# Prompt attention: score products and the steps of the sums over v traced one by one in turn

## The chip, the cores and the metric

The kernel runs on one core of a Trainium2 chip. The metric is the device time of one execution in microseconds (us). The core has five engines with a queue of instructions each: TensorE (PE, matrix products; its weight loads are listed as PEld), VectorE (DVE), ScalarE (ACT), GpSimd (POOL) and SyncE (SP, which issues most DMA transfers).

## What is computed

One inference step of a decoder with two layers, for a prompt of 2048 tokens and for 8 samples of 4 new tokens. Layer 0 joins a gated linear attention and a "forgetting" softmax attention of 4 heads of 128 channels, layer 1 is a gated linear attention. The change touches the softmax attention of the prompt alone, in the reference:

```python
def fox_prompt(q, k, v, log_f):                       # (1, 2048, 4, 128)
    c = jnp.cumsum(log_f, axis=1).swapaxes(1, 2)
    def block(args):                                  # 128 queries at a time
        qi, ci, s0 = args
        logits = einsum('bthd,bshd->bhts', qi, k) * scale + ci[..., None] - c[:, :, None, :]
        logits = where(t[:, None] >= key_pos[None, :], logits, -inf)
        p = softmax(logits, axis=-1)
        return einsum('bhts,bshd->bthd', p, v)
```

Beside it the kernel computes `fox_sample`, the same attention of the 32 sample tokens over a paged cache of 2048 past tokens for each sample.

## The kernel before

**The phase.** The program has three phases, one after the other: the input projections and linear attention of layer 0 (`phase_even`), the softmax attention (`phase_fox`, 877 to 1319 us of the profiled execution), and the output projection of layer 0 with all of layer 1 (`phase_odd`).

**Groups and blocks.** The prompt's attention goes through 16 groups (h, G): head h = 0 to 3, and in it G = 0 to 3, the 512 queries from 512 G on. A group has four blocks b = 0 to 3 of 128 queries. `scores(h, G, b)` makes G + 1 products of the block's queries with 512 keys each (the last with 128 (b + 1) keys). A number in float32 is carried as the sum of two in float16, so each product is three matmuls (`mm3`, L467 to L469). The result lies in a PSUM tile `s`, of which there are two; VectorE adds the bias, keeps the running maximum and writes the tile `L` (L1200). When the block's last product is out, the softmax follows: the negative maximum (L1206), one exponential for each `L` on ScalarE (L1208), the reciprocal of the sum on VectorE (L1211, L1212), and the normalisation of each `L` on GpSimd (L1216). `L` tiles lie in 17 buffers ("P").

**The sums over v.** `values(h, G, rows, po, b1, b2)` is a generator of steps. A full step (all four blocks, 128 keys) transposes up to four 128 x 128 pieces of `L` on TensorE into one PSUM tile `pt` (L1236), ScalarE rounds it to float16 (`th`, L1243), VectorE writes the rest (`tl`, L1244), and one `mm3` adds the product with v into the PSUM tile `po` (named fo), of which there is one. The transposes run two steps ahead of the matmuls. After the last step VectorE multiplies by the gate (`fy`, L1259) and GpSimd issues the store (L1261). A group has 4 (G + 1) such steps. The last group, (3, 3), is done in two halves, blocks 0 and 1 and then blocks 2 and 3, in 7 and 8 steps of two blocks and 256 keys each; a flag `alone`, read when a generator of sums starts, lets its transposes use two more PSUM tiles ("kt") when the sample attention is already traced.

**The order of tracing.** In a group's loop the sums of the group before (`pv`, `ns` = their number of steps) are dealt out over the blocks: for each block first `scores`, all its products and its softmax, then ns // 4 steps of `pv` (L1280 to L1283). So a block of G = 3 is traced as four products, softmax, three steps; of G = 2 as three products, softmax, two steps; of G = 1 as two, softmax, one; of G = 0 as one, softmax, and four steps of the last group of the head before. After the last block of (3, 3) come its two halves of sums, one after the other (L1288 to L1290).

**What merges with it.** Each `yield` gives a cost. `until` (L92) traces the prompt's generator and that of the sample attention so that their costs run as 270000 to 411000, until the sample's is done; the rest of the prompt is merged by `mux` (L75) with `prepare` (L1834) as 18000 to 12200. `prepare` splits the first unit of the output projection's weights into float16 (L345 to L350) and loads and splits the first two pieces, 256 tokens each, of that projection's input (L1592 to L1597).

**The engines' queues.** The order of tracing is not yet that of an engine. A planner goes through the program with costs of its own: of the instructions of an engine whose inputs and buffers it takes to be ready, it puts the one that was traced first into the queue. The chip then takes each queue in that fixed order.

Of the kernel before, what the change touches and what calls it, by code (L numbers as in the profile page):

```python
# [8 lines left out]
F32 = mybir.dt.float32  # L9
# [10 lines left out]
P = 128  # L20
# [101 lines left out]
class Kern:  # L122
# [1027 lines left out]
    def fox_prompt(self, fx, pps, caus):  # L1150
# [13 lines left out]
        def loads(h, G):  # L1164
            gs = slice(G * 512, (G + 1) * 512)
            raw["q"] = self.load(fx, self.qTd[h][:, gs], f"q{h}{G}")
            raw["k"] = self.load(fx, self.kTd[h][:, gs], f"k{h}{G}")
            bias(h, G)
            raw["v"] = self.load(fx, self.vd[gs, h * P : (h + 1) * P].rearrange("(c s) d -> s c d", s=P), f"v{h}{G}")
            SG[h, G] = fx.tile([P, 512], F32, tag="sg", name=f"fsg{h}{G}")  # L1170
            nc.sync.dma_start(SG[h, G], self.sgd[h][:, gs])

        def split(which, h, G):

            with ExitStack() as st:
                for x in (self.last_exp, self.last_kt):
                    if x is not None:
                        st.enter_context(self.tc.issue_after(x.ins))
                r = self.split(fx, raw[which], f"{which}{h}{G}", self.fsc["v", h // 2][0] if which == "v" else None)
                {"q": Q, "k": K, "v": V}[which][h, G] = r  # L1180

        def scores(h, G, b):
            tb = 4 * G + b
            cb = cbs[h]
            cm = fx.tile([P, P], F32, tag="cm", name=f"cm{h}{tb}")
            self.last_cm = nc.gpsimd.tensor_tensor(cm, cb[:, tb * P : (tb + 1) * P], caus, ALU.add)
            mx = fx.tile([P, 8], F32, tag="st1", name=f"mx{h}{tb}")
            L, na = [], 0
            q = [x[:, b * P : (b + 1) * P] for x in Q[h, G]]
            for j in range(G + 1):  # L1190
                w = 512 if j < G else (b + 1) * P
                ps = pps.tile([P, 512], F32, tag="s", name=f"s{h}{tb}{j}")
                self.last_pe = self.mm3(ps[:, :w], q, [x[:, :w] for x in K[h, j]], True, True)
                lt = fx.tile([P, 512], F32, tag="P", name=f"L{h}{tb}{j}")
                L.append((lt, w))
                parts = [(0, 512, cb[:, j * 512 : j * 512 + 512])] if j < G else \
                    ([(0, b * P, cb[:, j * 512 : j * 512 + b * P])] if b else []) + [(b * P, (b + 1) * P, cm)]
                for a, e, bs in parts:
                    init = -3e38 if na == 0 else mx[:, na - 1 : na]
                    self.last_l = nc.vector.tensor_tensor_reduce(lt[:, a:e], ps[:, a:e], bs, 1.0, init, ALU.add,  # L1200
                                                                 ALU.max, mx[:, na : na + 1])
                    na += 1
                yield 3 * w / 2.4
            nm = fx.tile([P, 8], F32, tag="st1", name=f"nm{h}{tb}")
            ib = self.logit[h // 2][0]
            nc.vector.tensor_scalar(nm[:, 0:1], mx[:, na - 1 : na], ib, -1.0, ALU.mult, ALU.mult)  # L1206
            for j, (lt, w) in enumerate(L):
                self.last_exp = nc.scalar.activation(lt[:, :w], lt[:, :w], AF.Exp, bias=nm[:, 0:1], scale=ib,  # L1208
                                                     accum_out=nm[:, 2 + j : 3 + j])
            if G:  # L1210
                nc.vector.reduce_sum(nm[:, 1:2], nm[:, 2 : 3 + G], axis=mybir.AxisListType.X)  # L1211
                nc.vector.reciprocal(nm[:, 1:2], nm[:, 1:2])  # L1212
            else:
                nc.vector.reciprocal(nm[:, 1:2], nm[:, 2:3])
            for lt, w in L:
                nc.gpsimd.tensor_scalar(lt[:, :w], lt[:, :w], nm[:, 1:2], 2.0**14, ALU.mult, ALU.mult)  # L1216
            return L

        def values(h, G, rows, po, b1, b2):

            ns, per = 4 * G + b2, 4 // (b2 - b1)
            c1, c2 = b1 * P, b2 * P
            alone = self.sample_done

            def turn(j):


                tag = "kt" if alone and j % 2 else "t"
                pt = pps.tile([P, 512], F32, tag=tag, name=f"pt{h}{G}{b1}{j}")
                w, parts = 0, []  # L1230
                for s in range(j * per, min(j * per + per, ns)):
                    b0 = max(b1, s - 4 * G)
                    w = max(w, b0 * P if per == 1 else 0)
                    parts.append((s, w, b0 * P))
                    for b in range(b0, b2):
                        nc.tensor.transpose(pt[:, w : w + P], rows[b][s // 4][0][:, (s % 4) * P : (s % 4 + 1) * P],  # L1236
                                            self.ident)
                        w += P
                th = fx.tile([P, 512], F16, tag="th", name=f"th{h}{G}{b1}{j}")
                tl = fx.tile([P, 512], F16, tag="tl", name=f"tl{h}{G}{b1}{j}")  # L1240
                a = parts[0][1]
                self.turns.append((
                    nc.scalar.activation(th[:, a:w], pt[:, a:w], AF.Copy),  # L1243
                    nc.vector.tensor_tensor(tl[:, a:w], pt[:, a:w], th[:, a:w], ALU.subtract)))  # L1244
                return th, tl, parts

            nj = -(-ns // per)
            ahead = [turn(j) for j in range(min(2, nj))]
            for j in range(nj):
                if j + len(ahead) < nj:  # L1250
                    ahead.append(turn(j + len(ahead)))
                th, tl, parts = ahead.pop(0)
                for s, a, c0 in parts:
                    vv = [x[:, (s % 4) * P : (s % 4 + 1) * P] for x in V[h, s // 4]]
                    self.last_pe = self.mm3(po[:, c0:c2], vv, [x[:, a : a + c2 - c0] for x in (th, tl)], s == 0,
                                            s == ns - 1)
                yield sum(c2 - c0 for _, _, c0 in parts) * 2.1
            y = fx.tile([P, 512], F32, tag="y", name=f"fy{h}{G}{b1}")
            nc.vector.scalar_tensor_tensor(y[:, c1:c2], po[:, c1:c2], self.v_undo[h // 2], SG[h, G][:, c1:c2], ALU.mult,  # L1259
                                           ALU.mult)  # L1260
            nc.gpsimd.dma_start(self.yT[0][NH + h][:, G * 512 + c1 : G * 512 + c2], y[:, c1:c2])  # L1261

        groups = [(h, G) for h in range(NH) for G in range(4)]
        loads(0, 0)
        for x in "qkv":
            split(x, 0, 0)
        pv, ns = iter(()), 0
        for j, (h, G) in enumerate(groups):
            rows = []
            for b in range(4):  # L1270
                rows.append((yield from scores(h, G, b)))
                if j + 1 < len(groups):
                    if b == 0:
                        loads(*groups[j + 1])
                    elif b == 2:
                        split("q", *groups[j + 1])
                        split("k", *groups[j + 1])
                    elif b == 3:
                        split("v", *groups[j + 1])
                for _ in range(ns // 4):  # L1280
                    c = next(pv, None)
                    if c:
                        yield c  # L1283
            yield from pv
            po = pps.tile([P, 512], F32, tag="o", name=f"fo{h}{G}")
            if j + 1 < len(groups):
                pv, ns = values(h, G, rows, po, 0, 4), 4 * (G + 1)

        yield from values(h, G, rows, po, 0, 2)
        yield from values(h, G, rows, po, 2, 4)  # L1290

    def strips(self, makers, sources):
# [668 lines left out]
```

## Time and profile before

| | us |
|---|---|
| median of three runs | 2410.35 (2403.77 to 2413.72) |
| the profiled execution | 2408.25 |
| its span, first to last instruction | 2405.8 |
| the softmax phase in it | 877 to 1319 |
| TensorE busy in the span | 2296.7 (95%) |
| ScalarE, VectorE, GpSimd busy | 1111.1, 1418.9, 744.1 |

All rows are of the profiled execution. A row of a stretch tells how long each engine was busy in it, and the granted share of TensorE's full clock. A row of waits names the engine, the line and the tile that waited, and the instruction that it waited for. In a list in order of time, a row in square brackets tells how long the engine had been idle before it and what ended that. TensorE's instructions overlap, so the time that one takes from the stream is the distance of two starts, not the duration.

### The profile page before, as it was taken

What the parts mean: (1) busy time and instruction counts of PE and PEld (TensorE: products, weight loads), DVE (VectorE), ACT (ScalarE), POOL (GpSimd) and SP (SyncE); (2) the same over time, 40 slices, a digit from 0 to 9 for tenths busy, and PEclk for the clock granted to TensorE, in tenths of its full rate; (3) what the DMA queues carried; (4) which work ended last, traced back from release to release, by engine and by line L of the source; (5) the groups of instructions that cost most, each with busy time, mean ns of one, the idle gap of its engine ahead of it and who ended that gap; (6) DMA issues with size and microseconds to landing.
All of it is one profiled execution on the core that took longest, in us unless ns stands there. A gap on an engine that the chain in (4) does not pass through costs nothing. (4 is left out here: it accounts for less than half of the span.)

```text
span 2405.8 us, 58659 instructions
## 1 busy us (share of the span) xinstructions
PE 2296.7 (95%) x23324; PEld 1635.3 (68%) x23324; DVE 1418.9 (59%) x3345; ACT 1111.1 (46%) x2466; POOL 744.1 (31%) x839
## 2 busy tenths in 40 slices
PE   7999999999999999999997999999999999999998
PEld 5667668854655876655445876777678766666887
DVE  7556556546764548567667363665675644557554
ACT  6434243342433127466668254535443645545333
POOL 2233223112212225144465111432452222322222
PEclk9999999999999999999999999999999999999999
DMA  6231235435431276776865532122146312114453
GB/s 181 78 87 58 85 121 160 144 108 149 144 116 59 82 223 220 259 246 208 265 195 181 163 108 59 45 76 89 50 147 194 114 37 73 43 58 159 152 190 148
DMA packets 297013, 317.25 MB, mean 132 GB/s; under 512 B 39729, under 2 KB 241010, under 8 KB 296738
## 3 DMA queue, kind: packets, MB, share of 16 engines
q1 hardware_dynamic: 295234, 308.98, 40.7%
q8 instruction: 183, 3.00, 0.5%
q0 software_dynamic: 1504, 4.52, 0.5%
q14 instruction: 92, 0.75, 0.1%
HBM read 242.31 MB, written 71.11 MB: 130 GB/s over the span
## 5 line engine op out<-in xcount | busy, mean ns | idle before, releaser
L469 PE MATMUL pt_o<-w_o,act 128*128 128x256 f16 x1024 | 281.2, 275 | 4.1 <-DVE act L1597 3.9
L467 PE MATMUL pt_o<-w_o,act 128*128 128x256 f16 x1024 | 281.5, 275 | 2.4 <-ACT sg1C L523 2.4
L468 PE MATMUL pt_o<-w_o,act 128*128 128x256 f16 x1024 | 281.2, 275 | 0.0
L467 PEld LDWEIGHTS <-act 128*128 128x128 f16 x2304 | 226.9, 98 | 37.0 <-ACT act L462 4.7
L469 PEld LDWEIGHTS <-act 128*128 128x128 f16 x2304 | 226.8, 98 | 35.2 <-DVE act L1597 5.1
L468 PEld LDWEIGHTS <-act 128*128 128x128 f16 x2304 | 227.0, 99 | 33.6 <-issue 3.7
L467 PE MATMUL pt_Cv<-w_Cv,act 128*128 128x256 f16 (+1 forms) x512 | 140.3, 275 | 1.7 <-ACT act L462 0.9
L468 PE MATMUL pt_Cv<-w_Cv,act 128*128 128x256 f16 (+1 forms) x512 | 140.0, 274 | 0.0
L469 PE MATMUL pt_Cv<-w_Cv,act 128*128 128x256 f16 (+1 forms) x512 | 139.7, 274 | 0.0
L633 POOL TENSOR_TENSOR kA<-kA,fA 128x512 f32<-128x512 f32 (+1 forms) x56 | 79.0, 1411 | 191.6 <-PE gl_A L599 141.3
L1208 ACT ACTIVATE L<-L,nm,kc 128x512 f32<-128x512 f32 (+3 forms) x160 | 118.2, 740 | 37.9 <-DVE nm L1206 33.7
L633 POOL TENSOR_TENSOR kC<-kC,fC 128x512 f32<-128x512 f32 (+1 forms) x56 | 82.0, 1465 | 151.9 <-PE gl_C L599 112.5
L1216 POOL TENSOR_SCALAR L<-L,nm 128x512 f32<-128x512 f32 (+3 forms) x160 | 98.5, 629 | 65.3 <-DVE nm L1212 24.1
L1243 ACT ACTIVATE th<-pt 128x512 f16<-128x512 f32 (+3 forms) x159 | 80.6, 526 | 61.0 <-PE pt L1236 60.2
L1244 DVE TENSOR_TENSOR tl<-pt,th 128x512 f16<-128x512 f32 (+3 forms) x159 | 94.8, 609 | 22.1 <-ACT th L1243 21.0
L1236 PE MATMUL pt<-ident,L 128*128 128x128 f32 x544 | 91.9, 280 | 6.3 <-POOL L L1216 3.2
L1236 PEld LDWEIGHTS pt<-ident,L 128*128 128x128 f32 x544 | 67.2, 144 | 35.7 <-DVE tl L1244 8.7
L1360 PEld LDWEIGHTS pkt<-ident,pgcache_fox_k 128*128 128x128 f32 x512 | 57.5, 141 | 42.6 <-issue 25.1
L1360 PE MATMUL pkt<-ident,pgcache_fox_k 128*128 128x128 f32 x512 | 74.7, 278 | 7.3 <-DVE kts L1364 5.2
L467 PE MATMUL pt_Av<-w_Ai,act 128*128 128x256 f16 x256 | 70.5, 276 | 2.5 <-ACT act L462 2.5
L467 PE MATMUL fo<-th,h_v 128*128 128x512 f16 (+3 forms) x174 | 59.4, 341 | 12.4 <-ACT th L1243 9.5
L468 PE MATMUL pt_Av<-w_Ai,act 128*128 128x256 f16 x256 | 70.4, 275 | 0.8 <-POOL w_Ai L350 0.8
(950 smaller groups left out, 6756.6 us busy)
## 6 DMA issues: line engine op xcount, KB each, us to landing
pgcache_fox_k<-in_cache_fox_k SPq DMA_DIRECT2D x128, 256.0 KB, 4.3
pgcache_fox_v<-in_cache_fox_v SPq DMA_DIRECT2D x128, 256.0 KB, 3.9
yr<-yT SPq DMA_DIRECT2D x16, 1024.0 KB, 6.1
nx<-in_x_prompt SPq DMA_DIRECT2D x16, 512.0 KB, 4.9
wr_Aqf<-in_w_in_even SPq DMA_DIRECT2D x64, 128.0 KB, 3.8
wr_o<-in_w_out_even SPq DMA_DIRECT2D x32, 256.0 KB, 4.5
wr_Cv<-in_w_in_odd SPq DMA_DIRECT2D x32, 256.0 KB, 3.9
wr_Cqk<-in_w_in_odd SPq DMA_DIRECT2D x64, 128.0 KB, 3.0
```

Source lines behind the costliest of these rows:

```text
L467: nc.tensor.matmul(ps, lh[0], rh[0], start=first, stop=False)
L468: nc.tensor.matmul(ps, lh[0], rh[1], start=False, stop=False)
L469: return nc.tensor.matmul(ps, lh[1], rh[0], start=False, stop=last)
L633: nc.gpsimd.tensor_tensor(kv[:, :, 0], kv[:, :, 0], t1.to_broadcast([P, nb, w]), ALU.mult)
L1208: self.last_exp = nc.scalar.activation(lt[:, :w], lt[:, :w], AF.Exp, bias=nm[:, 0:1], scale=ib, accum_out=nm[:, 2 + j : 3 + j])
L1216: nc.gpsimd.tensor_scalar(lt[:, :w], lt[:, :w], nm[:, 1:2], 2.0**14, ALU.mult, ALU.mult)
L1236: nc.tensor.transpose(pt[:, w : w + P], rows[b][s // 4][0][:, (s % 4) * P : (s % 4 + 1) * P], self.ident)
L1243: nc.scalar.activation(th[:, a:w], pt[:, a:w], AF.Copy),
L1244: nc.vector.tensor_tensor(tl[:, a:w], pt[:, a:w], th[:, a:w], ALU.subtract)))
L1360: nc.tensor.transpose(pk[:, j * P : (j + 1) * P], pgs[j][:, h * P : (h + 1) * P], self.ident)
```

## The change

For every group but the last, the products of a block and its share of steps are traced in turn, by a new generator `beside`: after the n-th of the G + 1 products come floor(n ns' / (G + 1)) - floor((n - 1) ns' / (G + 1)) steps, where ns' = ns // 4. The rest of `scores`, which is the block's softmax, comes after the last of these steps. For the last group the sums of (3, 2) are dealt out over blocks 0 and 1 alone (ns // 2 = 6 steps to each); before block 2 is traced, `po` is taken for the last group, and its first half of sums (blocks 0 and 1) becomes the generator that stands beside the products of blocks 2 and 3, up to 8 steps to a block. The second half follows after both, as before.

```diff
+        def beside(a, na, b, nb):
+
+            for n in range(1, na + 1):
+                yield next(a)
+                for _ in range(n * nb // na - (n - 1) * nb // na):
+                    c = next(b, None)
+                    if c:
+                        yield c
+            return (yield from a)
+
         pv, ns = iter(()), 0
         for j, (h, G) in enumerate(groups):
-            rows = []
+            rows, end = [], j + 1 == len(groups)
+            po = None
             for b in range(4):
-                rows.append((yield from scores(h, G, b)))
-                if j + 1 < len(groups):
+                if end and b == 2:
+
+                    yield from pv
+                    po = pps.tile([P, 512], F32, tag="o", name=f"fo{h}{G}")
+                    pv, ns = values(h, G, rows, po, 0, 2), 4 * (G + 1)
+                rows.append((yield from beside(scores(h, G, b), G + 1, pv, ns // 2 if end else ns // 4)))
+                if not end:
...
-                for _ in range(ns // 4):
-                    c = next(pv, None)
-                    if c:
-                        yield c
             yield from pv
-            po = pps.tile([P, 512], F32, tag="o", name=f"fo{h}{G}")
-            if j + 1 < len(groups):
+            if not end:
+                po = pps.tile([P, 512], F32, tag="o", name=f"fo{h}{G}")
                 pv, ns = values(h, G, rows, po, 0, 4), 4 * (G + 1)
-
-        yield from values(h, G, rows, po, 0, 2)
         yield from values(h, G, rows, po, 2, 4)
```

## Rows read from the trace of the kernel before

**Rows 1.** the page's first part: busy us, share of the span, instructions

```profile
PE 2296.7 (95%) x23324; PEld 1635.3 (68%) x23324; DVE 1418.9 (59%) x3345; ACT 1111.1 (46%) x2466; POOL 744.1 (31%) x839
```

**Rows 2.** busy time by stage; columns: stretch, length, engines, granted clock, DMA share, GB/s

```profile
877.00:1110.00 233.00, 218.77 (x1637) 138.24 (x1635) 159.24 (x475) 140.92 (x311) 93.47 (x153) 0.99 0.73 241
1110.00:1200.00 90.00, 85.21 (x553) 41.41 (x552) 63.10 (x214) 58.64 (x136) 47.06 (x72) 0.98 0.81 264
1200.00:1215.00 15.00, 10.75 (x55) 4.80 (x53) 7.51 (x24) 9.44 (x24) 10.41 (x15) 0.80 0.88 281
...
1280.00:1319.00 39.00, 25.67 (x184) 19.38 (x183) 27.58 (x65) 34.94 (x71) 20.19 (x23) 0.95 0.58 190
```

**Rows 3.** what TensorE waited for, 892 to 1110 us: total us, times, longest us

```profile
PE pkt L1360 <- DVE kts L1364: 5.2, 6, 2.2
```

**Rows 4.** what TensorE waited for, 1110 to 1280 us

```profile
PE fo L467 <- ACT th L1243: 2.6, 3, 1.8
PE pt L1236 <- DVE tl L1244: 2.4, 8, 0.4
PE pt L1236 <- POOL L L1216: 2.1, 1, 2.1
```

**Rows 5.** what TensorE waited for, 1280 to 1319 us

```profile
PE fo L467 <- ACT th L1243: 6.9, 4, 2.6
PE fo L468 <- DVE tl L1244: 3.3, 6, 1.0
PE fo L467 <- DVE fy L1259: 2.6, 1, 2.6
PE pt L1236 <- POOL L L1216: 0.5, 1, 0.5
```

**Rows 6.** TensorE in order of time, 1267 to 1269 us

```profile
1267.25 0.38 PE L467 MATMUL fo<-th,h_v 128*128 128x512 f16 x1
1267.46 0.38 PE L467 MATMUL s<-h_k,h_q 128*128 128x512 f16 x1
...
1267.90 0.38 PE L469 MATMUL s<-h_k,l_q 128*128 128x512 f16 x1
1268.11 0.60 PE L1236 MATMUL pt<-ident,L 128*128 128x128 f32 x4
1268.55 0.38 PE L468 MATMUL fo<-tl,h_v 128*128 128x512 f16 x1
```

**Rows 7.** TensorE in order of time at the end of group (2, 2)

```profile
1180.48 0.38 PE L467 MATMUL fo<-th,h_v 128*128 128x512 f16 x1 [1.76 <-ACT th L1243]
...
1183.77 0.63 PE L468 MATMUL fo<-tl,h_v 128*128 128x512 f16 x1
1184.19 0.63 PE L469 MATMUL fo<-th,l_v 128*128 128x512 f16 x1
```

**Rows 8.** TensorE in order of time at the end of group (2, 3)

```profile
1202.55 0.38 PE L469 MATMUL s<-h_k,l_q 128*128 128x512 f16 x1
...
1209.90 0.69 PE L1236 MATMUL pt<-ident,L 128*128 128x128 f32 x2 [2.09 <-POOL L L1216]
```

**Rows 9.** TensorE in order of time, the last group

```profile
1287.10 0.38 PE L469 MATMUL s<-h_k,l_q 128*128 128x512 f16 x1
1290.12 0.27 PE L467 MATMUL fo<-th,h_v 128*128 128x256 f16 x1 [2.64 <-ACT th L1243]
...
1298.81 0.27 PE L467 MATMUL fo<-th,h_v 128*128 128x256 f16 x1 [2.15 <-ACT th L1243]
...
1305.73 0.28 PE L467 MATMUL fo<-th,h_v 128*128 128x256 f16 x1 [2.56 <-DVE fy L1259]
...
1318.83 0.42 PE L467 MATMUL pt_o<-w_o,act 128*128 128x256 f16 x1
```

**Rows 10.** ScalarE in order of time, the last group

```profile
1294.46 0.81 ACT L1208 ACTIVATE L<-L,nm,kc 128x512 f32<-128x512 f32 x1
...
1302.54 0.72 ACT L1596 ACTIVATE act<-yr,kc 128x512 f16<-128x512 f32 x1 [1.89 <-DMA yr<-yT]
```

## The prediction

> **What bounds the kernel now.** I read the page's first part, then busy time by stage, then TensorE's waits in each stage, then the order of its instructions at the ends of groups. TensorE is busy for 95% of the span [rows 1], so only what shortens or lengthens its idle time, or its time at the lower clock, moves the end. The change alters one phase, 877 to 1319 us. There TensorE is idle for 14.2 us up to 1110, 4.8 us up to 1200, 4.3 us from 1200 to 1215, and 13.3 us (39.00 - 25.67) from 1280 on [rows 2]. The last stretch is the dearest, and another engine is close to full in it: ScalarE, 34.94 of 39 us. All that an order of tracing can win in the phase is these 37 us and what the clock loses beside them: in 1200 to 1215 it was granted 0.80, which is the lower level for 0.4 of 15 us and so 3 us lost [rows 2]; after an idle time of 1.76 us at the end of group (2, 2) two matmuls of 512 columns start 0.42 us apart, the level of 1.2 GHz, where they otherwise start 0.22 us apart [rows 6, 7].
>
> Who ends the waits differs. Up to 1110 us it is VectorE's copy of the sample's transposed keys, 5.2 us [rows 3]. From 1110 to 1280 it is th, tl and the normalised L [rows 4]. At the end th has 6.9, tl 3.3, fy 2.6 us and the normalisation 0.5 [rows 5].
>
> **The order that is there already.** Though the products of a block are traced together, TensorE's queue doesn't hold them together: a matmul of the sums, then a whole product, then a step's four transposes, then the sums again [rows 6]. The planner has put sums where a product's buffer wasn't ready. So the first part of the change writes down much of what stands in the queue.
>
> **Part 1, blocks of the first 15 groups.** No instruction is added or removed. By the formula, G = 3 turns from SSSS VVV into SS V S V S V (S a product, V a step), G = 2 from SSS VV into SS V S V, and G = 1 and G = 0 keep SS V and S VVVV. What moves everywhere is the softmax: it is traced after the block's steps, with it the splits and loads of the next group that follow the block (SP's loads pass up to four steps, but are wanted three blocks later).
>
> A product is three matmuls 0.22 us apart, 0.65 us; a full step is four transposes, 0.44 us, and the same 0.65 us, 1.09 us together [rows 6].
>
> The gain: products no longer come to VectorE in bursts, so tl and the key copies may be served sooner. At most that takes away what now waits for VectorE, 5.2 + 2.4 us [rows 3, 4], and the key copies follow the sample's own order, so I count 2 us.
>
> The loss: at the end of a group the next sums need the softmax of block 3. At the end of (2, 3) the last product began its third matmul at 1202.55 and the first transpose of a normalised L at 1209.90: 7.35 us, of which the last 2.09 idle [rows 8]. Steps of the old sums and the next products cover the rest. In the new order up to two steps of G = 3 and one of G = 2 stand ahead of the last product instead of behind it, and so no longer cover: 3 groups x 2 x 1.09 + 4 x 1.09 = 10.9 us (group (3, 3) is reckoned apart). With a fall of the clock of 2 us at each of three such ends it would be 17 us. Below, it is nothing, if the planner pulls the product forward as it does now. Since rows 6 show it pulling, I take a quarter, 3 us. The softmax's own move costs nothing as long as ScalarE has room, 141 of 233 and 59 of 90 us busy [rows 2]: a ready exponential passes the th not yet ready; without that cover each G = 0 end would wait for four steps, 4.4 us, at three heads, 13 us, the outer bound in place of the 10.9.
>
> So part 1 is +1 us, between -8 and +17.
>
> A rule of the Trainium skill weighs on this. Row: the sums' matmul at 1180.48 waited 1.76 us for th, and nothing behind it in the queue ran meanwhile [rows 7]. The page "TensorE: Matmul & The Clock Gate", section "The mechanism", says of matmuls: "strict FIFO, no reordering". By it every late V that is now fixed ahead of an S also holds that S, which is the rival on the slow side below; by the rows alone it happens only where the planner errs on readiness.
>
> **Part 2, the last group.** Counting the yields, the sample's costs sum to 325480, so it ends when the prompt stands at 325480 x 270000 / 411000 = 213800 of 233300. Before, that is the start of block 3 of (3, 3); after, block 2 with its first product and the first of the 15 half steps. The work left for TensorE after the sample is the same, some 26 us [rows 2]; what changes is what stands beside what. A half step has four transposes and six matmuls of 256 columns, as many columns as a full one: 1.09 us.
>
> - The wait of 2.64 us at 1290.12 [rows 9], when the products were out at 1287.10 and the first half's th was still behind others on ScalarE, plus the tl behind it (0.7 us): now eight products, 5.2 us, stand beside the first half. Gain 3.3 us.
> - Block 3's softmax. Before, the first half's seven steps (7.6 us) stood behind block 3 and covered it, and 2.15 us at 1298.81 and 0.5 us for the normalisation stayed open [rows 5, 9], because block 3's exponentials began only at 1294.46 [rows 10]. Now nothing is traced between this softmax and the second half. All 7.35 us of it open would be 4.7 more than now; none, if products are pulled ahead, 2.7 less. I take +1.5.
> - The wait for fy, 2.56 us at 1305.73 [rows 9]: the first half's gate multiplication stood late on VectorE, after a transfer for which ScalarE had waited 1.89 us [rows 10]. It now comes with block 2, and the second half a whole block later. Gain 2.5; but the transfer's wait itself may stand before a th: +1.
> - The first half's generator starts before the sample's end, so `alone` is false and two transpose buffers less serve it. Waits for tl in the normal steps are 2.4 us in 8 times, 0.3 each [rows 4]: seven steps 2.1 us at most, nothing at least; 0.7.
> - The second half's own th and tl waits stay: the rest of rows 5.
>
> Sum -3.3 + 1.5 - 2.5 + 1 + 0.7 = -2.6 us, between -9 (the first three gone: 3.3 + 2.7 + 2.6) and +7 (only the losses: 4.7 + 2.1). ScalarE, full to 34.94 of 39, gives a floor of its own: 4.1 us, unless work for later stages steps back.
>
> **Sum.** +1 - 2.6 = -1.6 us against the profiled execution's 2408.25, its span plus 2.45 us around it: 2406.7. The median shown is 2.1 us above that execution and the lowest run 4.5 below, so I forecast 2407.
>
> **Rivals.**
> - *Ends of groups uncovered (slower).* Place: the ends of G = 2 and 3, where the next sums wait for L normalised. Price: 10.9 us of cover gone, 6 us of clock, and the last softmax's 4.7 with the first half's gains lost: 2408.25 + 17 up to 2430, I name 2424. It decides where TensorE, after its last product, has less work ready than those 7.35 us. For: two such ends already show 1.8 and 2.1 us idle [rows 7, 8]. Against: rows 6.
> - *Both tails close (faster).* All of part 2's gain, 9 us, and 6 us of VectorE's waits: 2393. For: 13.3 us idle in one stretch, the largest of the phase. Against: ScalarE's 34.94 of 39, and products already mixed.
> - *It does not do what it says.* The planner's queues come out nearly as before, and the tail stays ScalarE's: 2408 to 2412, I name 2410. For: rows 6. Against: the last group's order does change, by a whole block.
>
> **How the numbers follow.** Forecast 0.47, its own range 2400 to 2417; slower rival 0.15; faster rival 0.20; nothing happens 0.18. About 0.5%, 12 us, can be told from no change, so faster is under 2398.3 and slower over 2422.4, against the median. Faster: 0.20 and 0.04 of the forecast, less 0.01: 0.23. Slower: most of 0.15 and 0.04 of the forecast: 0.18. Same: 0.59. Range: 2391 to 2425 takes in the rivals' named times and leaves out some 2 in 10.
>
> **What would show it.** Right: in the new profile the waits at the start of the first half (th) and before the second (fy) are gone from the last group, TensorE's idle time after the sample's end is 9 to 12 us, and the idle time from 892 to 1280 us is within 4 us of before. Wrong: waits for the normalised L of over 2 us at the ends of groups with G = 2 or 3 and a granted clock under 0.9 behind them (slow side); or the idle time of the whole phase under 22 us (fast side). Wrong in its ground: an output projection or a layer 1 that takes another time than before, which nothing here foresees.

## The result, and the profile after

The changed kernel takes 2412.43 us (median of 20 runs, 2406.54 to 2422.57), the kernel before beside it 2405.95 us (20 runs, 2398.41 to 2413.72): a ratio of 1.0035, 95% interval 1.0026 to 1.0045. The time lies 5.4 us above the forecast of 2407 and inside its range, but on the other side of no change: a loss of 6.5 us where 1.6 us of gain was forecast. The profiled execution has a span of 2413.4 us, before 2405.8.

The page's first part of the changed kernel (before: [rows 1]); the work is the same:

```profile
PE 2298.7 (95%) x23324; PEld 1636.7 (68%) x23324; DVE 1421.8 (59%) x3345; ACT 1111.2 (46%) x2466; POOL 745.9 (31%) x839
```

Four places in TensorE's queue can be found in every kernel here: the start of the softmax phase, one just ahead of the end of group (1,3), one in group (2,2), and the start of the last group, (3,3); the phase ends with the first matmul of the output projection. The work up to each is the same but for one matmul, and at the second place for 1.1 us of small ones, which the changed kernel has ahead of it. Busy time between the last four, kernel before (columns as in [rows 2]; the eighth, after the five engines, is the granted clock):

```profile
1119.20:1174.50 55.30, 53.44 (x353) 27.67 (x351) 42.18 (x147) 35.76 (x85) 31.41 (x48) 1.00 0.89 294
1174.50:1261.80 87.30, 80.15 (x482) 38.65 (x481) 55.77 (x189) 59.22 (x140) 47.31 (x73) 0.94 0.66 214
1261.80:1318.80 57.00, 43.39 (x298) 29.52 (x297) 43.96 (x111) 45.66 (x96) 29.35 (x38) 0.97 0.53 171
```

The same three stretches of the changed kernel:

```profile
1117.80:1179.80 62.00, 55.10 (x343) 27.87 (x344) 42.51 (x146) 40.28 (x95) 33.46 (x52) 0.94 0.81 269
1179.80:1264.80 85.00, 77.42 (x481) 37.73 (x481) 55.35 (x188) 58.86 (x139) 47.17 (x73) 0.98 0.62 201
1264.80:1324.30 59.50, 48.67 (x298) 31.82 (x297) 46.09 (x112) 49.56 (x102) 33.00 (x41) 0.86 0.57 180
```

The stretch with the end of (1,3) is 6.7 us longer, the one behind it 2.3 shorter, the last group 2.5 longer. Part of each is the clock: its loss, estimated as (1 - granted clock) x length, went from 0 to 3.7, from 5.2 to 1.7 and from 1.7 to 8.3 us.

What TensorE waited for in the changed kernel, 892 to 1110 us, 1110 to 1280, and 1280 to 1324 (total, times, longest; the same lines of code as in [rows 3 to 5], moved down by up to 10):

```profile
PE pkt L1370 <- DVE kts L1374: 6.5, 10, 2.2
...
PE pt L1236 <- POOL L L1216: 4.6, 2, 3.8
PE fo L467 <- ACT th L1243: 2.8, 3, 1.8
PE s L467 <- DVE mx L1200: 2.6, 6, 0.9
...
PE fo L467 <- ACT th L1243: 5.9, 3, 2.5
PE fo L468 <- DVE tl L1244: 2.1, 5, 0.6
PE pt L1236 <- DVE tl L1244: 1.2, 1, 1.2
```

The new wait is the one of 3.8 us for a normalised L. It stands at the end of (1,3), in order of time:

```profile
1107.07 5.34 PE L1509 MATMUL pv<-pgcache_fox_v,pT 128*16 128x512 f32 x48
...
1114.66 1.05 PE L1509 MATMUL pv<-pgcache_fox_v,pT 128*16 128x512 f32 x8
...
1117.11 0.38 PE L469 MATMUL s<-h_k,l_q 128*128 128x512 f16 x1
...
1118.97 0.28 PE L467 MATMUL s<-h_k,h_q 128*128 128x256 f16 x1 [0.86 <-DVE mx L1200]
...
1119.75 0.33 PE L469 MATMUL s<-h_k,l_q 128*128 128x384 f16 x1
1123.86 0.69 PE L1236 MATMUL pt<-ident,L 128*128 128x128 f32 x2 [3.79 <-POOL L L1216]
...
1126.66 0.63 PE L468 MATMUL fo<-tl,h_v 128*128 128x512 f16 x1
1127.09 0.63 PE L469 MATMUL fo<-th,l_v 128*128 128x512 f16 x1
```

Block 3's last product is the one at 1117.11; the products at 1118.97 and 1119.75 are already the next group's. Behind the wait two matmuls of 512 columns start 0.43 us apart, the level of 1.2 GHz, and the granted clock of these 10 us is 0.66:

```profile
1120.00:1130.00 10.00, 5.59 (x23) 2.13 (x23) 2.56 (x7) 5.85 (x15) 4.16 (x6) 0.66 0.86 289
```

In the kernel before the same place has no wait:

```profile
1112.18 0.38 PE L469 MATMUL s<-h_k,l_q 128*128 128x512 f16 x1
1112.49 3.63 PE L1499 MATMUL pv<-pgcache_fox_v,pT 128*16 128x512 f32 x32
1116.05 0.44 PE L1475 MATMUL ppt<-ident,pr 128*128 128x128 f32 x2
1116.42 1.91 PE L1499 MATMUL pv<-pgcache_fox_v,pT 128*16 128x512 f32 x16
...
1120.21 0.44 PE L1236 MATMUL pt<-ident,L 128*128 128x128 f32 x2
...
1120.93 0.38 PE L1236 MATMUL pt<-ident,L 128*128 128x128 f32 x2
```

GpSimd normalises block 3's L there, in the kernel before and in the changed one:

```profile
1119.86 2.70 POOL L1216 TENSOR_SCALAR L<-L,nm 128x512 f32<-128x512 f32 x4 [1.29 <-DVE nm L1212]
...
1123.12 3.04 POOL L1216 TENSOR_SCALAR L<-L,nm 128x512 f32<-128x512 f32 x5 [3.21 <-DVE nm L1212]
```

Of four L in 2.70 us the first is done at about 1120.5, so the first transposes that can read block 3 are those at 1120.93. Between the block's last product (1112.18) and them lay the sample attention's first steps over its own v (pv) and the transposes before them (ppt), 7.4 us of 8.1 of work. In the changed kernel these steps ran earlier, 48 of the matmuls ahead of the block's products and 8 between them, and 1.2 us of work was left. The softmax itself took no longer: from the last product to the first normalised L it is 6.7 us, in the kernel before 8.4. The cover of that end had been the sample's work, not the old sums'.

The last group of the changed kernel:

```profile
1290.96 0.22 PE L467 MATMUL fo<-th,h_v 128*128 128x128 f16 x1 [1.72 <-ACT th L1243]
...
1295.05 1.11 PE L1236 MATMUL pt<-ident,L 128*128 128x128 f32 x4 [1.21 <-DVE tl L1244]
...
1309.56 0.27 PE L467 MATMUL fo<-th,h_v 128*128 128x256 f16 x1 [2.49 <-ACT th L1243]
...
1316.85 0.49 PE L1236 MATMUL pt<-ident,L 128*128 128x128 f32 x3
1319.03 0.27 PE L467 MATMUL fo<-th,h_v 128*128 128x256 f16 x1 [1.69 <-ACT th L1243]
...
1324.24 0.27 PE L467 MATMUL pt_o<-w_o,act 128*128 128x256 f16 x1
```

The wait for fy (2.56 us in [rows 9]) is gone, as forecast, and so is the one of 2.64 us at the first half's start. Waits for th of 2.49 and 1.69 us stand late in the second half instead. What ScalarE did then:

```profile
1306.57 0.72 ACT L1606 ACTIVATE act<-yr,kc 128x512 f16<-128x512 f32 x1 [1.33 <-DMA yr<-yT]
...
1317.17 0.72 ACT L1602 ACTIVATE yr<-yr,kc 128x512 f32<-128x512 f32 x1
1317.78 0.72 ACT L345 ACTIVATE w_o<-wr_o,kc 128x512 f16<-128x512 f32 x1
1318.39 0.59 ACT L1243 ACTIVATE th<-pt 128x512 f16<-128x512 f32 x1
...
1322.09 0.75 ACT L348 ACTIVATE wr_Cv<-wr_Cv,kc 128x544 f32<-128x544 f32 x1
1322.72 0.49 ACT L1243 ACTIVATE th<-pt 128x384 f16<-128x384 f32 x1
```

Ahead of each th stand splits of the output projection's input (act, yr) and weights (w_o, wr_o), and even of layer 1's weights (wr_Cv). TensorE's last transposes for the sums, at 1316.85, were done by 1317.34; ScalarE took the last four th only from 1318.39 to 1322.72, with six splits started among them. The last experiments turn on this.

### The profile page after: what moved, and what is told of

It is laid out like the page before. It is cut to its first block, busy times and chain, and to the rows that moved or that the text cites. A ratio compares the mean times of both kernels' runs of the same rounds, so it can differ in the third digit from the quotient of the medians.

```text
span 2413.4 us, 58678 instructions
## 1 busy us (share of the span) xinstructions
PE 2298.7 (95%) x23324; PEld 1636.7 (68%) x23324; DVE 1421.8 (59%) x3345; ACT 1111.2 (46%) x2466; POOL 745.9 (31%) x839
## 5 line engine op out<-in xcount | busy, mean ns | idle before, releaser
L1236 PE MATMUL pt<-ident,L 128*128 128x128 f32 x544 | 93.8, 285 | 10.9 <-POOL L L1216 6.2
L467 PE MATMUL pt_Av<-w_Ai,act 128*128 128x256 f16 x256 | 70.7, 277 | 1.3 <-ACT act L462 1.3
L468 PE MATMUL pt_Av<-w_Ai,act 128*128 128x256 f16 x256 | 70.9, 277 | 0.8 <-POOL w_Ai L350 0.8
L469 PE MATMUL pt_Av<-w_Ai,act 128*128 128x256 f16 x256 | 70.5, 277 | 0.0
```

The costliest lines, as they stand in the source:

```text
L467: nc.tensor.matmul(ps, lh[0], rh[0], start=first, stop=False)
L468: nc.tensor.matmul(ps, lh[0], rh[1], start=False, stop=False)
L469: return nc.tensor.matmul(ps, lh[1], rh[0], start=False, stop=last)
```

## The experiments

The expectations call the theories by letters. A: ends of groups lost the work that covered their softmax. B: the new order of the last group carries the loss by itself. C: any other order of tracing mixes prompt and sample anew, and no part has a price of its own (C': the parts cost only together). D and E: the draw of chip or profile. F: ScalarE's later work sets the last group's length.

**What the runs gave.** Lengths come from the profiles (mean; the number of profiles stands in brackets), in us: from the start of the phase to the last group (front), in the last group, and their sum, the phase; "later work" counts ScalarE's instructions for later stages between the sixteenth th from the phase's end and the last one, in the queue. The ratio is that of the timed runs, each beside the kernel before on one chip; the chips differ from row to row, and the last row has 5 runs where the others have 11 to 20.

| kernel | front | last group | phase | later work | ratio to before, 95% interval |
|---|---|---|---|---|---|
| before (3 profiles) | 383.9 | 57.1 | 441.0 | 31 | |
| changed (3) | 389.6 | 59.6 | 449.2 | 35 | 1.0035 [1.0026, 1.0045]; again 1.0024 [1.0011, 1.0037], 1.0032 [1.0017, 1.0048] |
| part 1 alone (2) | 390.0 | 52.6 | 442.5 | 24 | 1.0004 [0.9989, 1.0019]; 1.0009 [0.9996, 1.0023] |
| part 2 alone (2) | 381.3 | 59.8 | 441.1 | 35 | 0.9997 [0.9983, 1.0010]; 1.0011 [0.9998, 1.0025] |
| softmax first (2) | 391.0 | 52.6 | 443.6 | 24 | 0.9986 [0.9974, 0.9997]; 0.9994 [0.9980, 1.0009] |
| softmax late (1) | 388.4 | 56.9 | 445.3 | 31 | 1.0011 [0.9998, 1.0024] |
| changed, (1,3) covered (2) | 386.8 | 61.2 | 448.0 | 37 | 1.0019 [1.0007, 1.0031] |
| changed, block 3 covered (2) | 390.0 | 56.9 | 447.0 | 30 | 1.0024 [1.0011, 1.0036] |
| softmax first, (1,3) covered (1) | 382.1 | 57.0 | 439.0 | 31 | 1.0002 [0.9990, 1.0014] |
| changed, later work behind (1) | 388.4 | 54.0 | 442.4 | 15 | 0.9992 [0.9982, 1.0002] |
| softmax first, covered, later work behind (1) | 385.2 | 51.3 | 436.5 | 18 | 0.9950 [0.9937, 0.9964] |

**The parts, one at a time.** Part 1 alone, `e1_alternate`: all blocks alternated by `beside`, the last group's sums as before.

```diff
-                rows.append((yield from scores(h, G, b)))
+                rows.append((yield from beside(scores(h, G, b), G + 1, pv, ns // 4)))
...
-                for _ in range(ns // 4):
-                    c = next(pv, None)
...
```

> The alternation alone: all groups traced product and step in turn, softmax, splits and loads behind the block's steps; the last group's two halves of sums stand behind its block 3, as before. Theory A (the ends of groups lost their cover): it carries the loss of the stage before the sample's end, 5 to 8 us slower than before, with a wait of over 2 us for the normalised L at an end of a group with G = 2 or 3. Theory B (the last group's edit carries the loss): within 3 us of before. Theory C (any new order of tracing re-mixes prompt and sample, no part has a price of its own): anywhere within 8 us, and not the sum's share.

Part 2 alone, `e2_last_group`: `beside` in the last group only, with the first half beside blocks 2 and 3.

```diff
+                if end and b == 2:
+                    yield from pv
+                    po = pps.tile([P, 512], F32, tag="o", name=f"fo{h}{G}")
+                    pv, ns = values(h, G, rows, po, 0, 2), 4 * (G + 1)
+                if end:
+                    rows.append((yield from beside(scores(h, G, b), G + 1, pv, ns // 2)))
+                    continue
...
```

> The last group's edit alone: the first 15 groups are traced as before (products, softmax, splits, steps), only group (3, 3) has six steps of the old sums beside each of blocks 0 and 1 and its first half of sums beside blocks 2 and 3. Theory A: within 3 us of before. Theory B: 4 to 6 us slower, with some 40 us or more from the sample's end to the first matmul of the output projection (44 in the changed kernel, 39 before), and a granted clock under 0.9 there. My forecast for this part was 2.6 us faster.

`e3_softmax_first`: products and steps in turn, but the block's last share of steps behind the softmax, the loads and the splits; last group as before.

```diff
-            for n in range(1, na + 1):
+            for n in range(1, na):
...
+                for _ in range(ns // 4 - G * (ns // 4) // (G + 1)):
```

> Alternation of the products, but the softmax and the splits and loads of a block stand right behind its last product, ahead of the step or steps that follow it; last group as before. Theory A in the form that the late softmax uncovers the ends: within 2 us of before. Theory A in the form that the late last product does it: as the alternation alone. Theory C: no relation to it.

`e4_softmax_late`: products together, then the steps, then softmax, loads and splits; last group as before.

```diff
+            for n in range(na):
+                yield next(a)
+            for _ in range(nb):
...
+            return (yield from a)
```

> Products of a block together as before, but softmax, splits and loads traced behind the block's steps; last group as before. Theory A in the form that the late softmax uncovers the ends: as slow as the alternation alone, 5 to 8 us over before, with the long wait for the normalised L at the end of (1, 2) or another end. In the form of the late last product: within 2 us of before. Theory C: no relation to it.

None of the four lies over 0.15% from no change, and the two parts added don't make the changed kernel's 1.0035: theories A and B, each of which put the loss into one part, fell as they were put. The profiles say more. In the queues, "softmax late" has part 1's order on TensorE up to group (2,2): there alternating the products adds nothing to tracing the softmax, the loads and the splits behind the steps. The changed kernel and all three with another front wait 3.8 us at (1,3), "softmax first" too, where only the block's last share of steps stands behind the softmax. What the three have in common is that steps of the old sums are traced ahead of the block's softmax; in "softmax first" that isn't separated from the order of the products.

**Do the parts add, and does the draw matter?** The changed kernel and three of the above again, first alone and then on one chip.

> The changed kernel once more, as it is. Part 1 alone and part 2 alone measured 1.0004 and 0.9997 of the kernel before, both parts 1.0035, although its queue is the one's up to the last group and the other's from there on. Theory A (ends of groups lost their cover; the prices stand) expects 1.002 to 1.004 again, in the profile TensorE's wait of 3.5 to 4 us for the normalised L at the end of group (1,3) and a granted clock of 0.80 to 0.90 in the 20 us behind it. Theory C (only the spread from one chip to another; no part has a price) expects 0.999 to 1.001, as the two parts gave.

> The changed kernel, on one chip with its two parts and the softmax-first order. Theory A (each part has the price that its stretch of the profile shows, some +6 us for part 1 and +3 for part 2): 1.0025 to 1.0035. Theory C' (the parts cost nothing alone, only both together): 1.0025 to 1.0035 as well, told apart by the two runs beside this one. Theory D (the sum depends on the chip): under 1.0015 here, where the parts were 1.000.

> Part 1 alone again (all blocks alternated, the last group's sums as in the kernel before). The profile gave 6.5 us more in the softmax phase, twelve timed runs 0.6 us. Theory A expects 1.001 to 1.0025; theory C' 0.9995 to 1.0005.

> Part 2 alone again (the last group's first half beside the products of its blocks 2 and 3, all else as in the kernel before). The profile gave 3.4 us more in the phase, twelve timed runs 1.3 us less. Theory A expects 1.0005 to 1.0015; theory C' 0.999 to 1.0.

> Products and steps in turn, the softmax ahead of the block's last share of steps, the last group as before, again. It measured 0.9986 on another chip, with an interval that left out 1. If that order is faster than the kernel before, 0.998 to 0.9993 here; if it was the draw of the runs, 0.9995 to 1.001. Theory A, which sees the same wait for L at the end of (1,3) in it, expects 1.000 to 1.002.

The changed kernel is slower each time, the parts are not: D falls. On the one chip the means of the spans are 7.9 us over the kernel before for the change, 1.4 for part 1 and 2.8 for part 2, with standard errors of 1.5, 1.1 and 1.0. The 3.7 us by which the whole exceeds the sum of its parts have one of 1.9 there, so the timed runs of this chip alone would not settle it. The profiles show where they don't add: part 1's front costs 6 us, and the old last group behind that front is 4.5 us shorter (52.6). With the new last group that is lost. The last group of part 1, second profile:

```profile
1266.40:1318.30 51.90, 43.62 (x298) 30.44 (x298) 41.09 (x109) 41.57 (x88) 27.93 (x37) 0.93 0.48 156
```

ScalarE has 88 instructions in it, 8 fewer than in the kernel before.

**Was the kernel before's profile typical?** Two more profiles of it, nothing changed.

> The kernel before, one look more. Theory A holds its softmax phase, from the first product to the first transpose of the output projection, to be 436 to 439 us again (437.7 in the profile shown, counted from the end of the input projections' queue), so that the changed kernel's 448 to 450 in three profiles is a loss of 10 to 12 us in the phase. Theory E (that profile was a lucky one in the phase) expects 440 to 443.

> The kernel before, a second look, for the same question: 436 to 439 us by theory A, 440 to 443 by theory E.

Phases of 440.9 and 444.4 us after the 437.7 of the profile that the prediction rests on: it had been the shortest of three, so the profiles' loss is 8 us, not the 10 to 12 that the first pair showed (theory E, in part). The second of the two also shows that the stretch with the end of (1,3) can lose time by itself, 3.9 us, with a wait for a page of the sample's v that came late, some 30 us behind that end, and a granted clock of 0.97 in place of 1.00:

```profile
1148.43 1.59 PE L1499 MATMUL pv<-pgcache_fox_v,pT 128*16 128x512 f32 x8 [2.22 <-DMA pgcache_fox_v<-in_cache_fox_v]
```

**Giving (1,3) its cover back.** In the changed kernel, hold the sample's steps until block 3's last product is out; 43 of 15327 matmuls move.

```diff
+                if b == 2 and (h, G) == (1, 3):
+                    yield -14000
...
+                if b == 3 and (h, G) == (1, 3):
+                    yield 14000
...
+                    st.enter_context(self.tc.issue_after(self.last_s.ins))
```

The two yields lower the prompt's cost by 14000 ahead of block 2 and give it back behind block 3, so that `until` traces more of the prompt there before the sample goes on. The last line, with `last_s` the prompt's latest product, holds the transposes (ppt) and the first four steps over v.

> The changed kernel, with one thing beside: in group (1,3) the sample attention's first steps over v and the transposes before them are kept back until block 3's last product is out. By the queue, 43 of TensorE's 15327 matmuls change their place, and the work between that last product and the first transpose of block 3's L grows from 1.2 to 5.1 us (the kernel before has 8.1). Theory A expects the wait of 3.8 us for L at that end to fall under 0.8 us, the clock behind it to stay over 0.95, and with both 4 to 7 us less than the changed kernel beside it: 1.000 to 1.002 of the kernel before. Theory C (the loss isn't tied to this place) expects the time of the changed kernel within 2 us, whether the wait goes or not, and the lower clock in other places.

> The changed kernel with the sample's steps kept back at the end of (1,3), a second look. The first had 3.2 us at the queue's stretch of (1,3) where the changed kernel has 6.5 to 7.8 over the kernel before, and 2 us more than that one in the stretch behind, where the clock fell in the first look. Theory A expects the 3 to 4 us at (1,3) again; if the clock's fall behind it was chance, the stretch behind is back at -2.5.

First profile, TensorE at the place:

```profile
1124.39 0.44 PE L1236 MATMUL pt<-ident,L 128*128 128x128 f32 x2 [0.56 <-POOL L L1216]
1125.40 0.57 PE L467 MATMUL fo<-th,h_v 128*128 128x512 f16 x1 [0.57 <-ACT th L1243]
```

The stretch around it in that profile:

```profile
1120.00:1130.00 10.00, 7.77 (x45) 2.94 (x38) 2.87 (x10) 6.08 (x15) 7.23 (x11) 0.83 0.95 331
```

And in the second, where the wait is 0.56 us again, the same matmul and the same stretch:

```profile
1125.41 0.38 PE L467 MATMUL fo<-th,h_v 128*128 128x512 f16 x1 [0.58 <-ACT th L1243]
...
1120.00:1130.00 10.00, 7.58 (x53) 3.42 (x46) 3.95 (x17) 6.87 (x17) 7.68 (x12) 1.00 0.86 293
```

The wait goes from 3.79 to 0.56 us, and the stretch with that end from 62.3 (mean) to 58.4 and 57.2. So the uncovered end, A's cause, is shown at this place. Its size for the whole isn't what A expected: the last group became 1.6 us longer (61.2), and of the 4 to 5 us, 1.3 are left in the timed means (1.0019 beside the changed kernel's 1.0024; the intervals overlap, so the timed runs alone don't show a gain).

**Giving the last group's block 3 its cover back.** Two of the first half's steps beside block 2, none beside block 3, the rest behind it.

```diff
-                rows.append((yield from beside(scores(h, G, b), G + 1, pv, ns // 2 if end else ns // 4)))
+                rows.append((yield from beside(scores(h, G, b), G + 1, pv,
+                                               (6, 6, 2, 0)[b] if end else ns // 4)))
```

> The changed kernel, with the last group's first half dealt out otherwise: two of its steps beside the products of block 2, none beside those of block 3, the rest behind block 3. By the queue the work between block 3's last product and the first transpose of its L is 4.5 us in place of 1.9. If the last group's loss is that cover and the clock that falls with it (theory A), the stretch from the end of group (3,1) to the last matmul of the phase is 2 to 4 us shorter than in the changed kernel, 0.9985 to 0.999 of it. If the loss is the old tail's waits in another place (theory B: any order of the last group pays), the time is that of the changed kernel within 1.5 us.

> The changed kernel with the last group's first half behind block 3, a second look. The first had 445.9 us for the phase in place of 448.3 to 450.3. Theory A expects 445 to 447 again, theory B 448 to 450.

The last group takes 57.1 and 56.8 us, 2.7 less, as A expected; the timed ratio, 1.0024, is that of the changed kernel beside it. It doesn't tell A from F: this order also has 30 instead of 35 instructions of later work. The same repair of (1,3) in the "softmax first" order gave the best front, 382.1 us, but lost that order's short last group (57.0 in place of 52.6), and timed no better:

> The order with the softmax ahead of a block's last share of steps and the last group as in the kernel before, which measured 0.9986 of it, with the sample's steps kept back at the end of (1,3) as in the run beside (cover 5.1 us in place of 1.0). It differs in 73 matmuls of TensorE's queue from that order. Theory A expects another 4 to 6 us off: 0.996 to 0.9975. Theory C expects 0.9985 again.

**What sets the last group's length.** In the table it rises with the column "later work": 24: 52.6; 30 and 31: 57; 35: 59.7; 37: 61.2, whatever was done at block 3. The changed kernel with and without (1,3) covered even has one and the same order of TensorE in the last group. So that work was put behind the last th in the changed kernel and in "softmax first, (1,3) covered", with TensorE's order left (8 and 3 of 15327 matmuls move).

```diff
+                self.last_th = nc.scalar.activation(th[:, a:w], pt[:, a:w], AF.Copy)
...
             for steps in pieces[2:]:
-                for step in steps:
-                    step()
+                steps[0]()
+                with self.tc.issue_after(self.last_th.ins):
+                    for step in steps[1:]:
+                        step()
...
+            with self.tc.issue_after(self.last_th.ins):
+                drain(dense(0, 3))
```

> The changed kernel, with the output projection's later work (its input from the third piece of 256 tokens on, and the splits of its further weights) put behind the last th of the prompt's sums. ScalarE's queue then holds 15 instead of 35 instructions of that work between the 16th th from the end and the last; of TensorE's 15327 matmuls 8 change their place. In the profiles so far the last group's length goes with that number: 24 of them 52.6 us, 30 and 31 some 57, 35 59.6, 37 61.2, some 0.65 us each. Theory F (the last group's th wait behind this work on ScalarE, so its price is set by how much of it the planner puts there) expects 47 to 53 us for the last group in place of 59.6, and 5 to 10 us less than the changed kernel for the whole, 0.9985 to 1.001 of the kernel before, less if the later stage then waits for its weights. Theory A (block 3's cover sets it) expects 59 to 60 us again and 1.0025 to 1.0035.

> The same put behind the last th, in the order with the softmax ahead of the last share of steps, the old last group, and the sample's steps kept back at the end of (1,3); 18 instead of 31 such instructions on ScalarE. Without it this order had 382 us up to the last group and 57.0 in it. Theory F expects 48 to 52 us in the last group, and for the whole 5 to 9 us less than the 1.0002 measured for it: 0.9965 to 0.998 of the kernel before. Theory A expects 57 us and 1.000.

The changed kernel with it, busy time in the last group:

```profile
1268.30:1322.30 54.00, 46.88 (x298) 32.00 (x297) 41.55 (x107) 39.26 (x83) 26.25 (x35) 0.87 0.53 172
```

What TensorE waited for longest in that stretch, in total:

```profile
PE fo L467 <- ACT th L1242: 3.4, 2, 1.7
```

ScalarE near its end:

```profile
1317.87 0.60 ACT L1242 ACTIVATE th<-pt 128x512 f16<-128x512 f32 x1 [1.32 <-PE pt L1236]
1319.09 0.60 ACT L1242 ACTIVATE th<-pt 128x512 f16<-128x512 f32 x1 [0.62 <-PE pt L1236]
```

Now ScalarE waits for TensorE's transposes, the other way round. The last group is 5.6 us shorter, and where the changed kernel had 1.0024 to 1.0035 of the kernel before, this one has 0.9992 (on another chip; its interval overlaps none of the three). So it is shown that this work, standing ahead of the last th, set the last group's length. That it does so through ScalarE's queue is read from the rows, 5.9 us of waiting for th in the changed kernel and 3.4 with the edit: the edit holds back VectorE's and GpSimd's share too (from 12 to 6 and from 11 to 6 instructions over the same 16 th), and no run separates them. And theory F's line ends: 15 and 18 instructions gave 54.0 and 51.3, where 0.65 us each below 24 would have given 47 to 49. The clock (0.87) stays. The other kernel, the page's first part:

```profile
PE 2288.5 (96%) x23324; PEld 1631.1 (68%) x23324; DVE 1420.8 (59%) x3345; ACT 1111.8 (46%) x2466; POOL 745.7 (31%) x839
```

Its three stretches, as above:

```profile
1115.90:1173.00 57.10, 53.52 (x345) 27.31 (x346) 41.42 (x141) 38.35 (x91) 32.98 (x52) 1.00 0.83 276
1173.00:1260.50 87.50, 80.18 (x485) 38.55 (x488) 55.47 (x188) 58.88 (x140) 47.20 (x73) 0.94 0.63 202
1260.50:1311.70 51.20, 41.73 (x298) 29.54 (x298) 39.55 (x107) 38.52 (x82) 25.42 (x35) 0.97 0.47 154
```

It takes 2393.66 us beside 2406.62, 0.9950 [0.9937, 0.9964], and beats both. Its phase is 4.5 us under the kernel before's mean; from there to TensorE's last matmul it takes 1071.1 us, where the three profiles of the kernel before have 1074.0 to 1077.3. Most of the gain is the clock: by (1 - clock) x span its timed runs lose 9.6 us less than those of the kernel before beside them, of 13.0 us less span in the mean. Why the clock holds better isn't shown.

## Why the prediction was wrong, point by point

- **Base and bound.** Right that TensorE's idle time and its clock decide, and that the change acts in the phase. But the terms were measured against one profile whose phase was the shortest of three.
- **Part 1, the gain of 2 us.** Wrong: the waits for the sample's key copies are 6.5 us in place of 5.2, and the stretch up to the end of (1,3) is 2.3 us longer on the means (242.2, before 240.0), 1.1 of it work that moved ahead of the mark.
- **Part 1, the loss of 3 us.** This term failed first. The prediction counted steps of the old sums as the only cover of a group's end and spread a quarter of their 10.9 us over seven ends. In fact six ends wait for L for 0.84 us at most, and one lost its cover, where the sample's steps had been the cover: 3.8 us of waiting and 3.7 us of clock in the profile, 5.8 us on the means. Its own sign for the slow side, a wait for L of over 2 us with a granted clock under 0.9 behind it, is what the trace shows (3.79 us, and 0.66 behind it), and its sign for being right, idle time from 892 to 1280 us within 4 us of before, failed with 6.8 us more. 2.3 us come back behind it, where the wait of 2.09 us in [rows 8] shrank to 0.84 and the clock lost 3.5 us less. Part 1's front: +5.7 us, not +1.
- **"The softmax's own move costs nothing."** Wrong: moving softmax, loads and splits behind the steps, with the products together, gives the same TensorE order up to (2,2) and the same wait.
- **Part 2, -2.6 us.** The waits did what was forecast: 13.6 us became 10.6 to 11.4 in three profiles, fy's and the first half's are gone, "9 to 12 us" held. Two things were not in the sum. The clock lost 6.6 to 8.3 us in the last group in place of 1.7 to 2.3, so that the stretch is 2.5 us longer. And the order on ScalarE was taken as given: the prediction named the 34.94 of 39 us and "unless work for later stages steps back", and let it stand as a floor. It was the lever: the change let 35 instead of 31 such instructions ahead of the last th, and putting later work behind that th brought 5.6 us.
- **Additivity.** The sum took the parts one by one. Part 1 shortens the old last group by 4.5 us, with 24 instructions of later work on ScalarE in place of 31, and part 2 takes that away: alone they are worth about 1 us each, together 6.5.
- **The rivals.** "Ends of groups uncovered" was the nearest, with its place and mechanism right at one end of seven and its price, 16 us, more than double; its named 2424 also lies under its own lower bound, 2408.25 + 17 = 2425. "Both tails close" and "does not do what it says" fell: the last group's order changed and lost.

The Trainium skill's page "PSUM — Partial Sum Buffer", section "Engine vs sequencer instructions", says of ScalarE's queue, as of VectorE's and GpSimd's, that it is "strict FIFO". The trace agrees: the th at 1318.39, whose transposes were done by 1317.34, did not pass the split at 1317.78, which stood ahead of it, and TensorE waited 1.69 us for that th. The prediction weighed that rule for TensorE's queue alone; the engine on which it decided was ScalarE.

Still open: why the clock fell in one profile of the kernel with (1,3) covered and not in the other, why that repair made the last group 1.6 us longer beyond the two more instructions counted there, which engine's later work counts, and why the 2.2 us by which block 3's repair shortens the phase, and the 4.6 us of the repair of (1,3) in the "softmax first" order, don't show in the timed runs.

## What to carry to other kernels

Where a planner fills the queues, read the order that it made on each engine before and after, at the places where the next stage waits: the cover of a wait may be another stream's work, which any change of tracing can move away. Where the last consumer waits for a helper engine, count the work for later stages that stands ahead of it in that engine's queue, and tie that work behind the last instruction that is urgent. Two edits in one pipeline needn't add: measure them together, and take more than one profile before a few microseconds are put down to a stretch.

## What was not expected of the hardware

- Less waiting was slower. In the last group TensorE's waits fell by 2 to 3 us and the stretch grew by 2.5: TensorE was busy for 48.67 us in place of 43.39 with the same work, as the granted clock went from 0.97 to between 0.86 and 0.89. Over the whole, the timed runs of the changed kernel lost 6.2 us more to the lower clock than the kernel before beside them (mean over both repeats of (1 - clock) x span), of the 6.8 us by which their spans are longer.
- The same queue with the same waits to 0.01 us up to 1125.4 had a granted clock of 0.83 in one profile and 1.00 in the other (1120 to 1130 us, above): the matmul at 1125.4 took 0.57 us in one and 0.38 in the other. From (1,3) to the last group the two profiles differ by 3.4 us, 1.2 in the stretch with that end and 2.2 in the next.
- Three profiles of the kernel before put its phase at 437.7, 440.9 and 444.4 us, while its last group took 57.0, 57.1 and 57.3: the spread sits ahead of it, 2.4 to 2.9 us in the phase's first 46 us and, in one of them, 3.9 in the stretch with the end of (1,3).
